# Adding a token's two expert results: the first one scaled on ScalarE and added on GpSimd, the embedding's copies on ScalarE

## The chip, the core and the metric

The kernel runs on one core of a Trainium2 chip. The metric is device time in microseconds of one execution. Before the change it is 1891.79 us, the median of three runs (1887.85 to 1893.83). Engines are named as the profile names them: PE is TensorE (PEld its weight loads), DVE is VectorE, ACT is ScalarE, POOL is GpSimd, SP is the engine that issues most DMAs.

## The reference

The program is a transformer block on 512 tokens of width 1024 (two attentions, a mixture of 32 experts, a gated per-layer embedding), and then two more layers with attention over a context. What the change touches lies where the experts' results are added and the embedding is mixed in:

```python
h = h + hier_moe(rms_norm(h, g_ffn[i]), w_rg[i], w_re[i], w1[i], w3[i], w2[i])
h = h + rms_norm(p[i] @ w_ple[i], g_ple[i]) * jax.nn.sigmoid(rms_norm(h, g_plg[i]) @ w_plg[i])
```

In `hier_moe` each token has two experts (TOP_K = 2), and its result is the sum of both expert outputs, each times the token's weight for that expert. So, for every token, h2 = h + w0*y0 + w1*y1; then the gate is a projection of the normalised h2, and u is the normalised embedding p @ w_ple.

## The kernel before

The 512 tokens are four chunks (c = 0 to 3) of 128 partitions, with the 1024 features along the free axis. The experts wrote their results to `y_d` in DRAM. When the last expert is done, `fetch(c)` (lines 1577 to 1582) gathers two tiles yk of a chunk by indirect DMAs that POOL issues, k = 0 and 1. Then a loop over chunks (lines 1586 to 1597) issues the gathers of the next chunk, adds both results into the chunk's tile h2 by two VectorE instructions (line 1591), takes the row norm (`row_norm`, line 404: a square with an accumulator on ACT at line 407, then in `rsq` a scaling on DVE at line 194 and a power on POOL at line 196), multiplies by the norm and the gain (`scaled`, line 410: tile xp), and turns xp for the matmul (`make_X`, line 381: transposes on PE at line 153, the high part Xhi on ACT at line 390, the low part Xlo on DVE at line 182). These high and low parts of a chunk, X, are what the gate's projection `b_plg` multiplies: three products per 128 features (`chunk`, line 257).

The loop also draws from a generator of filler work at line 1597. What is left there is `ple()` (line 1493): the embedding. A chunk's two halves of 512 columns come from PE into PSUM, are copied to the tiles pu (line 1502, called us in the code), squared on ACT (line 1508), and scaled on DVE (lines 1509 to 1513). The copy goes through `copy` (line 175), which counts an estimated load for ACT and DVE (`held`) and gives each copy to the one that has less. Each such copy so moves the count on which all later copies are shared out.

Each of the engines takes its instructions in a fixed order. That order is made when the program is built, by a scheduler that simulates all of it: neither the order of lines nor the engine's load at run time sets it. Beside the loop POOL has the low parts wlo of the gate's weights to make (line 251, 128x1024 each, from the high parts whi that ACT makes at line 242). The names with numbers below are buffers: h_9013 to h_9016 are the chunks 0 to 3 of h2; t_9411 and t_9418 are the two PSUM tiles of chunk 1's transposes (t_9413 and t_9420 after the change).

Of the kernel before, what the change touches and what calls it, by code (L numbers as in the profile page):

```python
# [16 lines left out]
AF = mybir.ActivationFunctionType  # L17
OP = mybir.AluOpType
# [64 lines left out]
def block_kernel(ctx: ExitStack, tc: tile.TileContext, I, out, dbg=None):  # L83
    nc = tc.nc
# [19 lines left out]
    def SM(shape, tag, dt=F32, bufs=2):  # L104
        return sm.tile(shape, dt, name=tag, tag=tag, bufs=bufs)
# [60 lines left out]
    def share(**us):  # L166

        e = min(us, key=lambda e: held[e] + us[e])
        busy(**{e: us[e]})
        return eng[e]  # L170

    def kcols(ap):
        return math.prod(ap.shape[1:]) / 1000

    def copy(o, i, on=("act", "dve")):

        us = dict(act=0.06 + 0.83 * kcols(o), dve=0.07 + 1.04 * kcols(o))
        e = share(**{n: us[n] for n in on})
        (e.copy if e is nc.scalar else e.tensor_copy)(o, i)  # L179
# [11 lines left out]
    def rsq(ssq, n, inv_n, pool=True):  # L191

        m, y, u = (SM([P, n], t, bufs=3) for t in ("rs_m", "rs_y", "rs_u"))
        nc.vector.tensor_scalar(m, ssq, inv_n, EPS, op0=OP.mult, op1=OP.add)
        if pool and n <= 4:
            nc.gpsimd.tensor_tensor(y, m, mhalf.to_broadcast([P, n]), op=OP.pow)
            return y
        nc.vector.tensor_scalar(y.bitcast(I32), m.bitcast(I32), 1, None, op0=OP.logical_shift_right)
        nc.vector.tensor_scalar(y.bitcast(I32), y.bitcast(I32), -1, 0x5F3759DF, op0=OP.mult, op1=OP.add)
        for _ in range(3):  # L200
            nc.vector.scalar_tensor_tensor(u, m, -0.5, y, op0=OP.mult, op1=OP.mult)
            nc.vector.tensor_mul(u, u, y)
            nc.vector.scalar_tensor_tensor(y, u, 1.5, y, op0=OP.add, op1=OP.mult)
        return y
# [176 lines left out]
    def make_X(y, nk, dst=None):  # L381

        hi, lo = dst or (XT([P, nk, P], F32R, name=s) for s in ("Xhi", "Xlo"))
        for k0 in range(0, nk, 4):
            kn = min(4, nk - k0)
            ps = T1()
            for k in range(kn):
                tr(ps[:, k * P:(k + 1) * P], y[:, k0 + k::nk])
            pv = ps[:, :kn * P].rearrange("p (k t) -> p k t", k=kn)
            nc.scalar.copy(hi[:, k0:k0 + kn], pv)  # L390
            sub_lo(lo[:, k0:k0 + kn], pv, hi[:, k0:k0 + kn])
        return hi, lo

    def make_Xs(ys, nk):

        per = 1024 // (nk * P)
        X = []
        for c, y in enumerate(ys):
            if c % per == 0:
                t = [Y([P, min(per, len(ys) - c), nk, P], F32R, name=s) for s in ("Xhi", "Xlo")]  # L400
            X.append(make_X(y, nk, [u[:, c % per] for u in t]))
        return ByTok(X)

    def row_norm(x, n):

        ssq = SM([P, 1], "ssq1", bufs=4)
        nc.scalar.activation(junk[:, :n], x, AF.Square, accum_out=ssq)
        return rsq(ssq, 1, 1.0 / n)

    def scaled(y, x, r, g):  # L410

        nc.vector.scalar_tensor_tensor(y, x, r, g, op0=OP.mult, op1=OP.mult)
# [1070 lines left out]
    def ple_load():  # L1483
        if not xp:
            gp.append(Y([P, D], name="gple"))
            gp.append(load_row(gp[0], I["g_ple"], D))
            for c in range(NC4):
                x = T2([P, 256], name="px")
                load(x, I["p"][rows(c), :])
                xp.append(x)  # L1490


    def ple():
        wpv = I["w_ple"].rearrange("(p c) n -> p c n", c=2)
        blks = [Dense(wpv, 2, [(b * 512, 512)]).load().split() for b in range(2)]
        ple_load()
        gp[1]()
        Xp = make_Xs(xp, 2)
        yield
        for b, d in enumerate(blks):  # L1500
            d.X = Xp
            d.evac = lambda c, ps, b=b: copy(us[c][b], ps)
        for c in range(NC4):
            us.append([(K3 if c < 3 else T2)([P, 512], name="pu") for _ in range(2)])
            ssq = SM([P, 2], "ussq")
            for b in range(2):
                blks[b].chunk(c)
                nc.scalar.activation(junk[:, :512], us[c][b], AF.Square, accum_out=ssq[:, b:b + 1])
            nc.vector.tensor_tensor(ssq[:, 0:1], ssq[:, 0:1], ssq[:, 1:2], op=OP.add)
            r = rsq(ssq[:, 0:1], 1, 1.0 / D)  # L1510
            nc.vector.tensor_scalar(r, r, 0.5, None, op0=OP.mult)
            for b in range(2):
                scaled(us[c][b], us[c][b], r, gp[0][:, b * 512:(b + 1) * 512])
            yield
# [3 lines left out]

    us, paid = [], [0]
    filler = chain(ctx_path(cx), ple())  # L1520
    last = None
    ws = {0: early[0],
# [16 lines left out]
    _, wts, yidx, oidx, ovf_e, novf = res  # L1539
# [35 lines left out]
    yks = []  # L1575

    def fetch(c):
        for k in range(2):
            yk = Y([P, D], name="yk")
            i = k * NC4 + c  # L1580
            gather(yk, y_d.rearrange("b s n -> (b s) n"), yidx[:, i:i + 1])
            yks.append(yk)
# [3 lines left out]
    for c in range(NC4):  # L1586
        h = h2[c]
        if c + 1 < NC4:
            fetch(c + 1)
        for k in range(2):  # L1590
            nc.vector.scalar_tensor_tensor(h, yks[2 * c + k], wts[:, k, c:c + 1], h, op0=OP.mult, op1=OP.add)
        dbg(f"h2_{c}", h)
        r = row_norm(h, D)
        x = Y([P, D], name="xp")
        scaled(x, h, r, gplg)
        Xt.append(make_X(x, 8))
        next(filler, None)
# [356 lines left out]
```

## Time and profile before

| | us |
|---|---|
| runs, median (lowest to highest) | 1891.79 (1887.85 to 1893.83) |
| the profiled execution, its own time | 1893.7 |
| the profiled execution, its span from first to last instruction | 1891.9 |
| PE, DVE, ACT, POOL busy | 1683.8, 933.2, 741.0, 614.2 |

The span is 1.8 us shorter than the time of the same execution. Times in the rows are counted from the start of the span, so that a stretch can be found again in each view. Busy time is a sum over the whole span. What a change is worth depends on the stretch in which it lies, and on which engine there is waited for.

### The profile page before, as it was taken

What the parts mean: (1) busy time and instruction counts of PE and PEld (TensorE: products, weight loads), DVE (VectorE), ACT (ScalarE), POOL (GpSimd) and SP (SyncE); (2) the same over time, 40 slices, a digit from 0 to 9 for tenths busy, and PEclk for the clock granted to TensorE, in tenths of its full rate; (3) what the DMA queues carried; (4) which work ended last, traced back from release to release, by engine and by line L of the source; (5) the groups of instructions that cost most, each with busy time, mean ns of one, the idle gap of its engine ahead of it and who ended that gap; (6) DMA issues with size and microseconds to landing.
All of it is one profiled execution on the core that took longest, in us unless ns stands there. A gap on an engine that the chain in (4) does not pass through costs nothing. (4 is left out here: it accounts for less than half of the span.)

```text
span 1891.9 us, 28397 instructions
## 1 busy us (share of the span) xinstructions
PE 1683.8 (89%) x10457; PEld 1204.5 (64%) x10457; DVE 933.2 (49%) x2017; ACT 741.0 (39%) x1620; POOL 614.2 (32%) x697
## 2 busy tenths in 40 slices
PE   7999878969998889898897699898989989879988
PEld 6787655756655545455553578775556977757767
DVE  5755657353223122221332865566552757786652
ACT  5344547312222212121222444255562534656660
POOL 4861223212221212122112534533123436453232
PEclk9999988979999999998898899999999989999999
DMA  8445676688999999997999533100023435421031
GB/s 238 156 175 179 203 236 202 223 320 308 377 409 400 336 382 339 358 318 263 352 409 387 193 102 116 56 1 1 1 90 122 137 122 167 123 87 56 23 134 45
DMA packets 189983, 385.34 MB, mean 204 GB/s; under 512 B 28184, under 2 KB 86136, under 8 KB 189840
## 3 DMA queue, kind: packets, MB, share of 16 engines
q1 hardware_dynamic: 186384, 375.08, 56.1%
q0 software_dynamic: 3456, 8.39, 1.4%
q8 instruction: 84, 1.38, 0.3%
q14 instruction: 59, 0.48, 0.1%
HBM read 348.86 MB, written 38.13 MB: 205 GB/s over the span
## 5 line engine op out<-in xcount | busy, mean ns | idle before, releaser
L150 PE MATMUL d<-we,exT 128*64 128x256 f32 x2048 | 254.8, 393 | 10.9 <-DMA we<-in_w 8.0
L150 PE MATMUL d<-whi,Xhi 128*128 128x512 f32 (+2 forms) x560 | 219.1, 393 | 5.9 <-DVE gsg L587 3.4
L150 PE MATMUL d<-wlo,Xhi 128*128 128x512 f32 (+2 forms) x560 | 218.7, 391 | 3.5 <-POOL wlo L251 3.5
L150 PE MATMUL d<-whi,Xlo 128*128 128x512 f32 (+2 forms) x560 | 219.2, 392 | 1.3 <-DVE Xlo L182 1.2
L251 POOL TENSOR_TENSOR wlo<-raw,whi 128x1024 fp32r<-128x1024 f32 (+2 forms) x71 | 171.3, 2432 | 139.1 <-ACT whi L242 79.7
L150 PEld LDWEIGHTS d<-we,exT 128*64 128x64 f32 x2048 | 148.0, 140 | 101.2 <-issue 25.5
L242 ACT CAST whi<-raw 128x1024 fp32r<-128x1024 f32 (+2 forms) x130 | 131.7, 1020 | 130.4 <-PE d L150 89.3
L513 DVE TENSOR_REDUCE ast<-s 128x1 f32<-128x768 f32 (+1 forms) x160 | 135.3, 848 | 92.0 <-PE s L150 90.1
L515 ACT ACTIVATE pr<-s,ast 128x768 f32<-128x768 f32 (+1 forms) x160 | 131.2, 821 | 58.1 <-DVE ast L513 54.7
L153 PE MATMUL t<-ident,pr 128*128 128x128 f32 x832 | 125.5, 283 | 13.9 <-DVE PT L179 6.8
L150 PE MATMUL s<-stk 128*128 128x256 f32 x448 | 120.4, 355 | 18.7 <-ACT pr L515 14.2
L248 POOL TENSOR_TENSOR wlo<-raw,whi 128x512 fp32r<-128x512 f32 (+2 forms) x69 | 82.2, 1221 | 145.0 <-ACT whi L242 82.9
L150 PE MATMUL d<-we,eth 128*64 128x512 f32 x512 | 122.0, 603 | 6.7 <-DVE eth L1433 6.7
L150 PEld LDWEIGHTS d<-whi,Xhi 128*128 128x128 f32 x560 | 108.2, 193 | 28.3 <-DVE gsg L587 3.6
L150 PEld LDWEIGHTS d<-wlo,Xhi 128*128 128x128 f32 x560 | 108.1, 193 | 24.3 <-POOL wlo L251 4.4
L150 PEld LDWEIGHTS d<-whi,Xlo 128*128 128x128 f32 x560 | 108.0, 193 | 22.0 <-DVE Xlo L182 2.2
L150 PE MATMUL d<-whi,ot 128*128 128x512 f32 x384 | 120.2, 392 | 1.4 <-DVE rT L1291 0.9
L153 PEld LDWEIGHTS t<-ident,pr 128*128 128x128 f32 x832 | 96.4, 144 | 37.2 <-DVE PT L179 10.9
L1425 DVE SCALAR_TENSOR_TENSOR eth<-eth,d 128x256 f32<-128x256 f32 x32 | 13.5, 421 | 169.6 <-ACT eth L1424 169.6
L150 PEld LDWEIGHTS s<-stk 128*128 128x128 f32 x448 | 70.5, 195 | 34.9 <-ACT pr L515 22.9
L1457 POOL DMA_INDIRECT xg<-xn_d,gidx x16 | 16.6, 1039 | 222.2 <-PE t L153 114.2
L150 PEld LDWEIGHTS d<-whi,ot 128*128 128x128 f32 x384 | 71.9, 188 | 18.7 <-issue 1.8
(475 smaller groups left out, 3191.8 us busy)
## 6 DMA issues: line engine op xcount, KB each, us to landing
we<-in_w SPq DMA_DIRECT2D x378, 512.0 KB
raw<-in_l_w_mod SPq DMA_DIRECT2D x48, 512.0 KB
raw<-in_l_w_in SPq DMA_DIRECT2D x64, 256.0 KB
raw<-in_w_in SPq DMA_DIRECT2D x24, 512.0 KB
raw<-in_l_w_out SPq DMA_DIRECT2D x24, 512.0 KB
raw<-in_l_w_in SPq DMA_DIRECT2D x16, 512.0 KB
y_d<-ey SPq DMA_DIRECT2D x64, 128.0 KB
bias<-bias SPq DMA_DIRECT2D x48, 128.0 KB
```

The costliest lines, as they stand in the source:

```text
L150: nc.tensor.matmul(o, l, r, start=start, stop=stop)
L153: nc.tensor.transpose(o, x, identr if x.dtype == F32R else ident)
L242: nc.scalar.copy(t, src)
L248: e.tensor_tensor(t, src[:, k], hi[k].bitcast(F32), op=OP.subtract)
L251: e.tensor_tensor(t, src, whole.bitcast(F32), op=OP.subtract)
L513: nc.vector.tensor_reduce(st[:, h:h + 1], ps, op=OP.max, axis=AX.X, negate=True)
L515: nc.scalar.activation(p, ps, AF.Exp, bias=st[:, h:h + 1], accum_out=sums[:, c, h:h + 1])
L1425: nc.vector.scalar_tensor_tensor(th[:, 256:], th[:, :256], 1.0, ps[:, :256], op0=OP.add, op1=OP.mult)
L1457: nc.gpsimd.indirect_dma_start(out=x, out_offset=None, in_=src, in_offset=bass.IndirectOffsetOnAxis(ap=idx, axis=0), bounds_check=src.shap ...
```

## The change

The copies of the embedding's halves from PSUM (8 of 128x512) go to ACT always; they no longer pass through `copy`, and so no longer count in its sharing. Of a chunk's two expert results, the first, y0, is multiplied by its weight in place on ACT, and added to h2 on POOL. The second, y1, is multiplied and added on DVE by one instruction as before.

```diff
@@ -1499,7 +1499,7 @@
         for b, d in enumerate(blks):
             d.X = Xp
-            d.evac = lambda c, ps, b=b: copy(us[c][b], ps)
+            d.evac = lambda c, ps, b=b: nc.scalar.copy(us[c][b], ps)
@@ -1587,8 +1587,10 @@
         if c + 1 < NC4:
             fetch(c + 1)
-        for k in range(2):
-            nc.vector.scalar_tensor_tensor(h, yks[2 * c + k], wts[:, k, c:c + 1], h, op0=OP.mult, op1=OP.add)
+        y0, y1 = yks[2 * c:2 * c + 2]
+        nc.scalar.activation(y0, y0, AF.Copy, scale=wts[:, 0, c:c + 1])
+        nc.gpsimd.tensor_tensor(h, h, y0, op=OP.add)
+        nc.vector.scalar_tensor_tensor(h, y1, wts[:, 1, c:c + 1], h, op0=OP.mult, op1=OP.add)
         r = row_norm(h, D)
```

In the changed kernel these lines are 1591 (scale), 1592 (add) and 1593 (the second result), and all lines behind them stand two lower.

POOL's order at the start of the loop, as a difference; cyk belongs to a side path, rs_y is the power of a norm, DMA yk a gather:

```order
 L756 TENSOR_TENSOR cyk<-cyk,g_8271 128x256 x2
 L196 TENSOR_TENSOR rs_y<-rs_m,mhalf 128x1
-L251 TENSOR_TENSOR wlo<-raw,whi 128x1024 x2
+L1592 TENSOR_TENSOR h_9013<-h_9013,yk 128x1024
+L251 TENSOR_TENSOR wlo<-raw,whi 128x1024 x2
+L1592 TENSOR_TENSOR h_9014<-h_9014,yk 128x1024
 L196 TENSOR_TENSOR rs_y<-rs_m,mhalf 128x1 x2
 L1457 DMA yk<-y_d,yidx 128x1024 x2
 L196 TENSOR_TENSOR rs_y<-rs_m,mhalf 128x1
 L1457 DMA yk<-y_d,yidx 128x1024 x2
```

The adds of chunks 0 and 1 stand around the two low parts, and all four ahead of the next powers and gathers.

DVE's order at the same place, before:

```order
L1591 SCALAR_TENSOR_TENSOR h_9013<-yk,wts,h_9013 128x1024
L179 COPY pu<-d_9428 128x512
L1591 SCALAR_TENSOR_TENSOR h_9013<-yk,wts,h_9013 128x1024
L1511 TENSOR_SCALAR rs_y<-rs_y 128x1
L1591 SCALAR_TENSOR_TENSOR h_9014<-yk,wts,h_9014 128x1024
L412 SCALAR_TENSOR_TENSOR pu<-pu,rs_y,gple 128x512 x2
L1591 SCALAR_TENSOR_TENSOR h_9014<-yk,wts,h_9014 128x1024
L194 TENSOR_SCALAR rs_m<-ssq_9335 128x1
L1509 TENSOR_TENSOR ussq<-ussq 128x1
L194 TENSOR_SCALAR rs_m<-ussq 128x1
L412 SCALAR_TENSOR_TENSOR xp<-h_9013,rs_y,gplg 128x1024
```

And after:

```order
L1511 TENSOR_SCALAR rs_y<-rs_y 128x1
L412 SCALAR_TENSOR_TENSOR pu<-pu,rs_y,gple 128x512 x2
L1593 SCALAR_TENSOR_TENSOR h_9013<-yk,wts,h_9013 128x1024
L194 TENSOR_SCALAR rs_m<-ssq_9336 128x1
L1509 TENSOR_TENSOR ussq<-ussq 128x1
L194 TENSOR_SCALAR rs_m<-ussq 128x1
L1593 SCALAR_TENSOR_TENSOR h_9014<-yk,wts,h_9014 128x1024
L412 SCALAR_TENSOR_TENSOR xp<-h_9013,rs_y,gplg 128x1024
```

The scaling of chunk 1's embedding (pu) stands ahead of chunk 0's h2 now, and chunk 1's h2 behind the two sums of norms.

DVE's order further on, after the change, where chunks 2 and 3 are added:

```order
L1593 SCALAR_TENSOR_TENSOR h_9015<-yk,wts,h_9015 128x1024
L1511 TENSOR_SCALAR rs_y<-rs_y 128x1
L412 SCALAR_TENSOR_TENSOR pu<-pu,rs_y,gple 128x512 x2
L194 TENSOR_SCALAR rs_m<-ssq_9468 128x1
L1593 SCALAR_TENSOR_TENSOR h_9016<-yk,wts,h_9016 128x1024
L182 TENSOR_TENSOR Xlo<-t_9420,Xhi 128x512
L412 SCALAR_TENSOR_TENSOR xp<-h_9015,rs_y,gplg 128x1024
```

Chunk 1's second low half (t_9420) stands behind chunk 3's h2 in both kernels; before, it stood behind xp of chunk 2 as well. Behind this place the orders differ in single neighbours only: about a dozen copies have changed between ACT and DVE in the later layers, by the count that no longer gets the embedding's copies.

## Rows read from the trace of the kernel before

**Rows 1.** The page of the profiled execution: its first line, the line of busy time by engine (us, share of the span, instructions), and the granted TensorE clock in 40 slices of 47.3 us (tenths of full speed).

```profile
span 1891.9 us, 28397 instructions
...
PE 1683.8 (89%) x10457; PEld 1204.5 (64%) x10457; DVE 933.2 (49%) x2017; ACT 741.0 (39%) x1620; POOL 614.2 (32%) x697
...
PEclk9999988979999999998898899999999989999999
```

**Rows 2.** The view of stretches: from:to in us of the span, its length, busy us and instructions of PE, its weight loads, DVE, ACT and POOL, then the granted TensorE clock, the share of the DMA engines and GB/s.

```profile
...
1060.00:1072.00 12.00, 0.21 (x1) 0.21 (x2) 11.55 (x14) 6.12 (x13) 6.82 (x6) 0.61 0.45 142
1072.00:1080.00 8.00, 6.11 (x21) 4.65 (x21) 5.30 (x9) 2.23 (x5) 6.47 (x6) 0.52 0.66 189
...
1090.00:1130.00 40.00, 38.41 (x179) 31.48 (x178) 27.50 (x29) 15.60 (x22) 15.51 (x8) 1.00 0.28 92
```

**Rows 3.** The timeline of PE from 1059 to 1092 us: start us, us, engine, line, operation, tiles, shape, count; in brackets the idle time before it and what ended that. The tile t is a transpose of a chunk's xp, d a product in the gate's projection (b_plg) or, at 1059.44, the last one of the embedding.

```profile
1059.44 0.39 PE L150 MATMUL d<-whi,Xlo 128*128 128x512 f32 x1
1071.79 1.97 PE L153 MATMUL t<-ident,xp 128*128 128x128 f32 x8 [11.96 <-DVE rs_y L1511]
...
1074.17 0.63 PE L150 MATMUL d<-wlo,Xhi 128*128 128x512 f32 x1
1076.69 1.12 PE L153 MATMUL t<-ident,xp 128*128 128x128 f32 x4 [1.89 <-DVE Xlo L182]
...
1085.24 0.50 PE L150 MATMUL d<-whi,Xlo 128*128 128x512 f32 x1 [0.51 <-DVE Xlo L182]
...
1089.63 1.22 PE L153 MATMUL t<-ident,xp 128*128 128x128 f32 x8 [1.36 <-DVE xp L412]
```

**Rows 4.** The timeline of DVE (VectorE) from 1055 to 1093 us, same columns; h is a chunk of h2, yk an expert result, pu half a chunk of the embedding.

```profile
1057.11 2.70 DVE L1591 SCALAR_TENSOR_TENSOR h<-yk,wts,h 128x1024 f32<-128x1024 f32 x1
1060.33 5.61 DVE L1591 SCALAR_TENSOR_TENSOR h<-yk,wts,h 128x1024 f32<-128x1024 f32 x1
...
1065.93 1.27 DVE L1591 SCALAR_TENSOR_TENSOR h<-yk,wts,h 128x1024 f32<-128x1024 f32 x1
1067.12 1.40 DVE L412 SCALAR_TENSOR_TENSOR pu<-pu,rs_y,gple 128x512 f32<-128x512 f32 x2
1068.44 1.27 DVE L1591 SCALAR_TENSOR_TENSOR h<-yk,wts,h 128x1024 f32<-128x1024 f32 x1
1069.64 0.14 DVE L194 TENSOR_SCALAR rs_m<-ssq 128x1 f32<-128x1 f32 x1
...
1069.88 0.15 DVE L194 TENSOR_SCALAR rs_m<-ussq 128x1 f32<-128x1 f32 x1
1070.45 1.28 DVE L412 SCALAR_TENSOR_TENSOR xp<-h,rs_y,gplg 128x1024 f32<-128x1024 f32 x1 [0.41 <-POOL rs_y L196]
...
1074.75 1.28 DVE L412 SCALAR_TENSOR_TENSOR xp<-h,rs_y,gplg 128x1024 f32<-128x1024 f32 x1 [1.24 <-POOL rs_y L196]
...
1081.92 2.66 DVE L1591 SCALAR_TENSOR_TENSOR h<-yk,wts,h 128x1024 f32<-128x1024 f32 x2 [2.43 <-DMA yk<-y_d,yidx]
```

**Rows 5.** The timeline of POOL (GpSimd) from 1055 to 1080 us, same columns; two instructions of a kind in a row are joined (x2).

```profile
1057.27 1.45 POOL L756 TENSOR_TENSOR cyk<-cyk,g 128x256 f32<-128x256 f32 x2
1058.66 1.57 POOL L196 TENSOR_TENSOR rs_y<-rs_m,mhalf 128x1 f32<-128x1 f32 x1
1060.21 4.64 POOL L251 TENSOR_TENSOR wlo<-raw,whi 128x1024 fp32r<-128x1024 f32 x2
1069.86 1.07 POOL L196 TENSOR_TENSOR rs_y<-rs_m,mhalf 128x1 f32<-128x1 f32 x2 [5.01 <-DVE ussq L1509]
1071.10 1.57 POOL L1457 DMA_INDIRECT yk<-y_d,yidx  x1 [0.17 <-POOL rs_y L196]
1072.98 1.13 POOL L1457 DMA_INDIRECT yk<-y_d,yidx  x1 [0.31 <-issue]
1074.13 0.58 POOL L196 TENSOR_TENSOR rs_y<-rs_m,mhalf 128x1 f32<-128x1 f32 x1
```

**Rows 6.** The timeline of POOL once more, at 1036 us and from 1123 to 1132 us: one low part made with VectorE idle beside it, and two of them in a row.

```profile
1036.60 2.34 POOL L251 TENSOR_TENSOR wlo<-raw,whi 128x1024 fp32r<-128x1024 f32 x1 [2.50 <-ACT whi L242]
...
1124.35 5.82 POOL L251 TENSOR_TENSOR wlo<-raw,whi 128x1024 fp32r<-128x1024 f32 x2 [2.79 <-ACT whi L242]
```

**Rows 7.** The timeline of DVE from 1123 to 1132 us, beside the two low parts of rows 6.

```profile
1123.40 1.22 DVE L251 TENSOR_TENSOR wlo<-raw,whi 128x1024 fp32r<-128x1024 f32 x1
1124.54 3.42 DVE L665 TENSOR_TENSOR ly<-ly,mrow 128x1024 f32<-128x1024 f32 x1
1127.87 2.84 DVE L1611 TENSOR_TENSOR h<-h,pth 128x512 f32<-128x512 f32 x1
```

**Rows 8.** The timeline of ACT (ScalarE) from 1066 to 1068 us, same columns.

```profile
1066.33 1.06 ACT L407 ACTIVATE junk<-h 128x1024 bf16<-128x1024 f32 x1 [4.93 <-DVE rs_y L1511]
1067.29 0.19 ACT L407 ACTIVATION_READ_ACCUMULATOR junk<-h 128x1 f32 x1
1067.51 0.63 ACT L1508 ACTIVATE junk<-pu 128x512 bf16<-128x512 f32 x1
```

**Rows 9.** The groups by line of the whole span, shapes kept apart: line, engine, operation, tiles, shape, count, busy us, mean ns of one, then the idle time of the engine ahead of them and what ended it.

```profile
L179 ACT COPY pu<-d 128x512 f32<-128x512 f32 x4 | 2.3, 586 | 2.1 <-PE d L150 2.1
...
L1591 DVE SCALAR_TENSOR_TENSOR h<-yk,wts,h 128x1024 f32<-128x1024 f32 x8 | 16.0, 1996 | 2.5 <-DMA yk<-y_d,yidx 2.4
...
L179 DVE COPY pu<-d 128x512 f32<-128x512 f32 x4 | 2.7, 685 | 0.2 <-PE d L150 0.2
```

## The prediction

> **What bounds the kernel now.** First the page: TensorE is busy for 1683.8 of 1891.9 us, all other engines for under half, so the span moves only where PE waits [rows 1]. The chain of waits reaches back only to 1140.70 us, behind the place of the change, so I read this place from the timelines, engine by engine. PE ends the embedding's last product at 1059.44 + 0.39 and stands still for 11.96 us, until chunk 0's xp is there for the transposes at 1071.79; then it waits 1.89 us for chunk 1's, 0.51 for a low part and 1.36 for xp of chunk 2 [rows 3]. From 1090 to 1130 us it is busy for 38.41 of 40 us [rows 2]. What these four waits (15.72 us) gain or lose is therefore carried to the end.
>
> What fills the 11.96 us? DVE: y0 of chunk 0 in 2.70 us, y1 in 5.61, chunk 1's two in 1.27 each, and pu between [rows 4]. Undisturbed such an instruction takes 1.27; the group's mean of 1.996 [rows 9] is no price of work. POOL makes two low parts beside them (1060.21, 4.64 us together) [rows 5]. One alone is 2.34 us [rows 6], so these two ran undisturbed and DVE's 5.61 is waiting: 1060.33 + 5.61 = 1065.94, which is 1.09 behind POOL's end at 1064.85. The two engines take turns where both read two tiles.
>
> How they do so decides this change. At 1124.35 two low parts take 5.82 us [rows 6], 1.14 more than 2 x 2.34, while a DVE addition beside them takes 3.42 and the next 2.84 [rows 7]: DVE waits to the end of the low part that runs, then gets in, and the next low part is longer by DVE's turn. At 1060.33 DVE was passed over at that boundary and waited through both.
>
> By the Trainium skill ("SBUF — State Buffer", "Who interferes with whom") a DVE instruction with two inputs in SBUF and a GpSimd instruction that reads SBUF lock each other out, for the whole instruction, and whoever issues first has the ports. The turns at 1124 agree. By that rule alone the 5.61 would have ended at about 1063.6, one boundary earlier; the row shows more than the rule.
>
> **The change, part by part.** *Removed from DVE*: four additions at 1.28 and four pu copies at 0.685 [rows 4, 9], less one gplg copy that goes to it: 5.1 + 2.7 - 0.7 = 7.2 us. Of this only what lies before 1070.45 could count, and there DVE waits for POOL anyway.
>
> *Added to ACT*: four copies at 0.586 [rows 9] and four scalings of 128x1024; none is in the trace, the nearest row is the square at 1.06 us [rows 8], so 1.1 each, in all 6.1 us after the gplg copy is off. ACT had 4.93 us idle ahead of 1066.33 [rows 8], and chunk 0's scaling can be done at about 1058, when POOL still has cyk and a power before it. I cost it at nothing. Bounds: 0, and 2 x 1.1 if that cover is gone (chunks 0 and 1 both late for POOL). No gain below nothing: it is work added.
>
> *Added to POOL*: four additions of 128x1024, two inputs in SBUF. The trace has no such addition on POOL; nearest is the low part of the same size, 2.34 us alone [rows 6]. I take that. Lower bound 1.27, DVE's own time for that size; upper 2.91, half of 5.82. These stand on the path: chunk 0's before both low parts, chunk 1's behind them, and all ahead of the powers and of chunk 2's two gathers.
>
> *Moved on DVE*: pu of chunk 1 stands before chunk 0's h2, and chunk 1's h2 behind the two sums of norms. So chunk 0's xp waits for DVE's h2 of chunk 1, and that waits for ACT.
>
> The sum for chunk 0 by turns: POOL's power ends at 1057.27 + 1.45 + 0.58 [rows 5], some 0.2 later because a copy on ACT delays what leads to it: 1059.5. POOL adds chunk 0's y0 until 1061.8; DVE scales half of pu (0.70) to 1062.5; low part to 1064.8; second half to 1065.5; low part to 1067.8; DVE adds y1 to 1068.9, where before it was 1065.94. POOL adds chunk 1's y0 to 1071.25. ACT squares h2 and two halves of pu: 1.25 + 2 x 0.82 with their accumulators [rows 8], 1071.8. DVE's small sums 0.14 + 0.15 and gaps [rows 4], 1072.2; chunk 1's y1, 1.27, 1073.5; xp, 1.28, 1074.8. PE begins at 1074.8, where before it was 1071.79: **+3.0**.
>
> *Second wait.* POOL's next power (0.58) ends at 1073, two gathers (1.57 + 0.31 + 1.13) and a power (0.58) [rows 5] end at 1076.6, chunk 1's xp, with issue, at 1078.1 instead of 1076.03 [rows 4]. PE, by then 3.0 late, would have been at the transposes at 1077.8 less its 1.89 of waiting: it waits less, and its shift there is **+1.5**. The TensorE clock stands here: 0.61 and 0.52 were granted from 1060 to 1080, after PE stood still [rows 2], and 1.00 from 1090. The longer stop and the shorter second one leave that as it is, so I charge nothing; bound +1.0 (a product is 0.63 us at 1074.17 against 0.39 [rows 3]: four more of them at the low level).
>
> *Third.* The gathers of chunk 2 go out 2 us later. DVE's h2 additions at 1081.92 waited 2.43 for a gather [rows 4], so chunk 2's y1 is added at 1083.9, ends at 1085.2. Then chunk 3: POOL's addition ends at 1089.1 (waiting for the gathers, then 2.34 and turns), DVE's at 1090.4, and behind it on DVE stands chunk 1's second low half, 1091.1; xp of chunk 2 comes next. PE's transposes of chunk 2 come at 1093.4 against 1089.63, +3.8. But in the new order about ten products of chunk 1 stand before them, 38.41 / 179 = 0.21 us each [rows 2], 2.2 us of work that PE had left to do later; and its waits on the late low half cost about 1.2. **+2.8 - 0.1**, so the sum at the end is **+2.7**.
>
> *Later layers.* About a dozen copies of at most 0.7 us change engine by the count. No row of this stretch prices this. PE runs there mostly without a wait [rows 1, 2]; I take 0, bounds -4 and +4: half a dozen copies at 0.685 on the path to either side.
>
> So span 1894.6, profiled execution 1893.7 + 2.7 = 1896.4. The median of the runs is 1.9 below that execution: **1894.5 us**. A measurement of this kernel can tell about 0.3% from no change, 5.7 us: below 1886.1 or above 1897.5.
>
> A rule speaks against the whole move: the Trainium skill ("Perfetto Trace Analysis", "Optimizing Scalar/DVE Operations") says that GpSimd and DVE share a read port, so that shifting work between them might not help. The sum above says the same from the rows: a DVE turn of 1.27 becomes a POOL turn of 2.34 that DVE must wait for.
>
> **The rivals.** *Passed over (slower).* If DVE loses every boundary in this train, as it did at 1060.33 [rows 4], four POOL instructions run unbroken, 1059.5 + 4 x 2.34 = 1068.9; pu twice (1.40) and y1 (1.27) follow, 1071.5; with 1.25 + 1.64 + 0.3 + 1.27 + 1.28 PE begins at 1077.3, +5.5, and one more lost turn at chunk 3's addition makes +6.5: **1898.3 us**. It decides from +5.7, so two lost boundaries and one more. For it: both rows of 2.70 and 5.61 lie in this very stretch. Against: at 1124 DVE got in at each boundary [rows 6, 7].
>
> *POOL alone bounds (faster).* If DVE's turns fit beside POOL's (pu ready before the train begins, additions shorter than 2.34), chunk 0's h2 is ready early and only POOL's 1068.9 + 0.6 counts: y1 of chunk 1 ends at 1070.2, xp at 1071.5, -0.3; the later waits of 0.51 and 1.36 [rows 3] vanish, since DVE has 7.2 us less to do: -2.2, **1889.6 us**. For it: relief of DVE, which is busy for 5.30 of 8 us at 1072 [rows 2]. Against: DVE's wait for POOL is most of its time there. All of the idle, 15.72, caps any gain.
>
> *Copies outweigh.* The copies shared out anew decide the sign, and the place matters little: **1887 to 1899 us**, middle 1893.
>
> **How the numbers follow.** By turns 0.45 (a change of +2.7, own range 1891 to 1898); passed over 0.22; POOL alone 0.20; copies 0.13. Faster by over 0.3%: a fifth of POOL alone, a third of copies, little of the rest: 0.11. Slower by over 0.3%: six tenths of passed over, a seventh of by turns, a third of copies: 0.25. Within: 0.64. The range goes from the low end of POOL alone with copies in its favour, 1887, to passed over with the clock's and copies' share, 1901.
>
> **What would show it.** In the profile after: PE's wait before the first transposes 15 us instead of 11.96 (step one); low parts longer than 2.34 with pu's turns between; DVE's y1 of chunk 0 ending near 1068.9; xp of chunk 1 near 1078; chunk 2's transposes near 1093.4, behind more products of chunk 1. It is wrong if DVE's pu or y1 waits over a boundary (passed over), if PE begins at or before 1071.8 (POOL alone), if POOL's addition is far from 2.34, or if the stretch up to 1095 shifts by one amount and the end by another (copies).

## The result and the profile after

The changed kernel takes 1910.25 us, the median of four runs (1907.12 to 1915.15), beside 1892.81 (four runs now, three before the prediction) for the kernel before: ratio 1.0096, 95% interval 1.0075 to 1.0117, so 14 to 22 us slower. The forecast was 1894.5 with a range from 1887 to 1901. The profiled execution took 1915.15 us.

The page of the changed kernel, with the lines that answer to [rows 1]:

```profile
span 1913.4 us, 28411 instructions
...
PE 1699.3 (89%) x10457; PEld 1213.5 (63%) x10457; DVE 927.7 (48%) x2005; ACT 746.6 (39%) x1632; POOL 621.0 (32%) x701
```

DVE is busy for 5.5 us less than before, ACT for 5.6 and POOL for 6.8 more; the prediction had 7.2 and 6.1 for the first two. (Busy time counts an instruction from start to end, so it includes what the instruction waits inside, such as the 10.20 us below.) The span is 21.5 us longer all the same. To see where, I compared the starts of the same matmul, by its number, in both traces (10457 in each). The table gives what each stretch of the program added to PE's delay against the first trace of the kernel before, in us; the stretches are named by that trace's times.

| trace | to 1059 | place, to 1095 | to 1512 | to 1526 | to 1626 | to the end | all behind the place |
|---|---|---|---|---|---|---|---|
| changed | +1.6 | +4.8 | +4.3 | +3.2 | +3.7 | +3.8 | +15.0 |
| changed, second trace | +9.3 | +4.1 | +0.5 | +3.1 | +3.9 | +1.1 | +8.6 |
| changed, third trace | +1.9 | +6.0 | +1.5 | +3.2 | +4.0 | +3.7 | +12.4 |
| before, second trace | -6.8 | +0.2 | -1.8 | 0.0 | -1.3 | +0.3 | -2.8 |

Up to 1048 us each engine has the same instructions in the same order in both kernels, and PE has them up to its stop at the place. The first column moves by at most 1.9 us behind 1048, so the rest of it is chance: the experts' part differs by 16 us between executions. The other columns are known better: the two traces of the kernel before differ there by at most 1.8 in one stretch and by 2.8 in the last column. The place costs 4 to 6 us, and the later layers, for which the prediction took 0 with bounds of 4, cost 9 to 15.

**The place.** PE's timeline, answering to [rows 3]:

```profile
1078.09 1.97 PE L153 MATMUL t<-ident,xp 128*128 128x128 f32 x8 [16.64 <-DVE rs_y L1511]
...
1083.10 1.12 PE L153 MATMUL t<-ident,xp 128*128 128x128 f32 x4 [1.76 <-DVE rs_m L194]
...
1094.70 0.50 PE L150 MATMUL d<-whi,Xlo 128*128 128x512 f32 x1 [0.50 <-DVE Xlo L182]
...
1097.13 1.05 PE L153 MATMUL t<-ident,xp 128*128 128x128 f32 x8
```

The wait before the first transposes is 16.64 us instead of 11.96. POOL's timeline of the same stretch, answering to [rows 5]:

```profile
1060.31 0.56 POOL L196 TENSOR_TENSOR rs_y<-rs_m,mhalf 128x1 f32<-128x1 f32 x1
1060.85 2.34 POOL L1592 TENSOR_TENSOR h<-h,yk 128x1024 f32<-128x1024 f32 x1
1063.16 4.63 POOL L251 TENSOR_TENSOR wlo<-raw,whi 128x1024 fp32r<-128x1024 f32 x2
1067.76 2.33 POOL L1592 TENSOR_TENSOR h<-h,yk 128x1024 f32<-128x1024 f32 x1
...
1075.71 1.54 POOL L196 TENSOR_TENSOR rs_y<-rs_m,mhalf 128x1 f32<-128x1 f32 x1 [1.16 <-DVE rs_m L194]
...
1090.21 2.51 POOL L1592 TENSOR_TENSOR h<-h,yk 128x1024 f32<-128x1024 f32 x1 [2.71 <-ACT yk L1591]
```

DVE's timeline, answering to [rows 4]:

```profile
1061.10 10.20 DVE L412 SCALAR_TENSOR_TENSOR pu<-pu,rs_y,gple 128x512 f32<-128x512 f32 x2
1071.22 1.27 DVE L1593 SCALAR_TENSOR_TENSOR h<-yk,wts,h 128x1024 f32<-128x1024 f32 x1
...
1075.55 1.28 DVE L1593 SCALAR_TENSOR_TENSOR h<-yk,wts,h 128x1024 f32<-128x1024 f32 x1
1076.75 1.28 DVE L412 SCALAR_TENSOR_TENSOR xp<-h,rs_y,gplg 128x1024 f32<-128x1024 f32 x1
...
1092.76 1.28 DVE L1593 SCALAR_TENSOR_TENSOR h<-yk,wts,h 128x1024 f32<-128x1024 f32 x1 [1.40 <-POOL h L1592]
1093.96 0.68 DVE L182 TENSOR_TENSOR Xlo<-t,Xhi 128x512 fp32r<-128x512 f32 x1
```

Read the two side by side. POOL's addition, two low parts and second addition take 2.34, 4.63 and 2.33 us, nothing more than alone, one right behind the other from 1060.85 to 1070.09: this is POOL's *train*. DVE's two scalings of pu, 1.40 in [rows 4], take 10.20: the first got its turn only when POOL was through, 1.2 us ahead of their joint end at 1071.30. It was passed over at three boundaries out of three. That is the rival "passed over", to the row. Behind it y1 of chunk 0 (1071.22), ACT's squares, y1 of chunk 1 (1075.55) and xp (1076.75) follow as in the sum. At the end of the stretch DVE's addition of chunk 3 waits 1.40 for POOL's, and chunk 1's last low half (1093.96) stands behind it; PE waits 0.50 for that half at 1094.70. The cover of the new work on ACT held, as ACT's timeline shows:

```profile
1058.11 1.16 ACT L1591 ACTIVATE yk<-yk,wts 128x1024 f32<-128x1024 f32 x1 [0.77 <-DMA yk<-y_d,yidx]
...
1060.11 1.06 ACT L242 CAST whi<-raw 128x1024 fp32r<-128x1024 f32 x1
1062.48 1.15 ACT L1591 ACTIVATE yk<-yk,wts 128x1024 f32<-128x1024 f32 x1 [1.32 <-DMA yk<-y_d,yidx]
```

The first scaling (1.16 us) ended at 1059.27, 1.6 us before POOL could use it.

The view of stretches, answering to [rows 2]:

```profile
1062.00:1078.00 16.00, 0.00 (x0) 0.00 (x0) 13.34 (x9) 6.23 (x11) 10.75 (x7) 0.64 0.29 95
1078.00:1086.50 8.50, 6.59 (x20) 4.97 (x21) 4.97 (x11) 4.21 (x9) 7.67 (x6) 0.50 0.70 192
1096.00:1136.00 40.00, 37.72 (x176) 30.81 (x174) 26.91 (x28) 15.43 (x22) 15.15 (x8) 1.00 0.28 92
```

The clock is low at the same place: 0.64 and 0.50 after PE stood still, 1.00 from 1096.

**The later layers.** The largest wait that is new stands at 1526 us (1512 to 1526 in the table), where the second layer's query latent yqa is normalised. PE's timeline of the changed kernel there:

```profile
1532.64 1.52 PE L153 MATMUL t<-ident,yqa 128*128 128x128 f32 x6 [5.99 <-DVE yqa L412]
```

ACT's timeline just ahead of it (whi is a weight's cast, junk a square):

```profile
1525.19 1.05 ACT L242 CAST whi<-raw 128x1024 fp32r<-128x1024 f32 x1 [5.23 <-DMA raw<-in_l_w_in]
1526.14 0.52 ACT L1744 ACTIVATE junk<-yqa 128x384 bf16<-128x384 f32 x1
...
1526.66 0.46 ACT L179 COPY yqa<-d 128x384 f32<-128x384 f32 x1
1527.15 0.52 ACT L1744 ACTIVATE junk<-yqa 128x384 bf16<-128x384 f32 x1
```

The low part on DVE that frees a buffer:

```profile
1518.92 2.36 DVE L251 TENSOR_TENSOR wlo<-raw,whi 128x1024 fp32r<-128x1024 f32 x1
```

The DMA queue (SPq), which fills that buffer:

```profile
1521.30 0.37 SPq L129 DMA_DIRECT2D raw<-in_l_w_in  x1
```

In the kernel before, PE's timeline at the same transposes:

```profile
1517.17 1.11 PE L153 MATMUL t<-ident,yqa 128*128 128x128 f32 x6 [1.28 <-DVE yqa L412]
```

Its ACT:

```profile
1508.77 0.49 ACT L179 COPY yqa<-d 128x384 f32<-128x384 f32 x1
...
1510.67 1.06 ACT L242 CAST whi<-raw 128x1024 fp32r<-128x1024 f32 x1 [0.60 <-DMA raw<-in_l_w_in]
```

And its DMA queue:

```profile
1507.07 0.37 SPq L129 DMA_DIRECT2D raw<-in_l_w_in  x1
```

Before, a copy of yqa and its square on ACT are done ahead of a weight's cast, which waits 0.60 us for its DMA. After, the cast waits 5.23, and two squares and the last copy are queued behind it; PE waits 5.99 instead of 1.28 (the prediction's rows do not reach here). The DMA went out at 1507.07 before, just when POOL's low part freed a buffer; after, at 1521.30, just when DVE's low part (1518.92 + 2.36) did. (POOL's low part, 1504.63 + 2.41, ended at 1507.04.) Nobody edited this code: four copies of yqa went to DVE, ACT, DVE, ACT where they had gone to ACT, DVE, ACT, DVE, and in the order that follows the transfer got another buffer. The section on the change says that behind the place the orders differ in single neighbours only. That is too little: compared by names, some 5% of PE's instructions behind 1130 us and 10 to 12% of DVE's and ACT's stand outside the longest order that both kernels share.

### The profile page after: what moved, and what is told of

Same layout as the page of the kernel before. It is cut to its first block, busy times and chain, and to the rows that moved or that the text cites. A ratio compares the mean times of both kernels' runs of the same rounds, so it can differ in the third digit from the quotient of the medians.

```text
span 1913.4 us, 28411 instructions
## 1 busy us (share of the span) xinstructions
PE 1699.3 (89%) x10457; PEld 1213.5 (63%) x10457; DVE 927.7 (48%) x2005; ACT 746.6 (39%) x1632; POOL 621.0 (32%) x701
## 5 line engine op out<-in xcount | busy, mean ns | idle before, releaser
L150 PE MATMUL d<-we,exT 128*64 128x256 f32 x2048 | 259.2, 398 | 9.7 <-DMA we<-in_w 6.8
L1457 POOL DMA_INDIRECT xg<-xn_d,gidx x16 | 16.6, 1036 | 223.2 <-PE t L153 114.6
```

The source lines that it names most:

```text
L150: nc.tensor.matmul(o, l, r, start=start, stop=stop)
L1457: nc.gpsimd.indirect_dma_start(out=x, out_offset=None, in_=src, in_offset=bass.IndirectOffsetOnAxis(ap=idx, axis=0), bounds_check=src.shap ...
```

## The experiments

Theory after the result: the loss has two parts, the **place** (POOL's train keeps DVE out) and the **sharing** (the count without the embedding's copies shares out all later copies in another way). Rival: the place carries all, and the later stretches are chance. The runs are called e1 to e16; differences in us are worked out from the ratios.

**1. Sharing alone (e1, and once more as e14).** The kernel before; the copies go where they went, uncounted.

```diff
-            d.evac = lambda c, ps, b=b: copy(us[c][b], ps)
+            d.evac = lambda c, ps, b=b: (nc.scalar.copy if (c < 2) == (b == 0) else nc.vector.tensor_copy)(us[c][b], ps)
```

> The kernel before, in which the embedding's eight copies go to the engines that they went to before (half to ACT, half to DVE), but no longer count in the sharing; nothing else is edited. The additions stand as before. Sharing theory (most of the loss is in the later layers, because every later copy is shared out by another count): PE keeps its time up to 1130 us and loses 9 to 13 us behind 1400 us; 1902 to 1906 us where the kernel before has 1893. Place theory (the expert additions and the copies' own move carry the loss, the later layers differ only by chance): 1893, within 3 us of the kernel before.

> The kernel before with the copies where they were, but uncounted, a second time. Parts that add up: 5 to 9 us over the kernel before. If its first measurement (6.8) was low by chance: 10 us or more.

Ratios 1.0036 (1.0016 to 1.0055) and 1.0074 (1.0053 to 1.0095): +6.8 and +14.0 us, with no instruction of the experts' results touched. The two intervals (3 to 10 and 10 to 18 us) barely meet.

**2. All but the sharing (e2, and once more as e15).** The changed kernel; the copies on ACT count as before.

```diff
-            d.evac = lambda c, ps, b=b: nc.scalar.copy(us[c][b], ps)
+            d.evac = lambda c, ps, b=b: (share(act=0.06 + 0.83 * 0.512, dve=0.07 + 1.04 * 0.512), nc.scalar.copy(us[c][b], ps))
```

> The changed kernel, in which the embedding's copies go to ACT but are counted as before, so that later copies are shared out as in the kernel before. Sharing theory: only the loss at the place is left, PE's first transposes of xp 5 us later than before and the end 4 to 7 us later; 1897 to 1900 us. Place theory: the whole loss, 1907 to 1913 us.

> The changed kernel with the copies counted as before, a second time. Parts that add up: 3 to 6 us over the kernel before. If its first measurement (3.6) was low by chance: 8 us or more.

Ratios 1.0019 (1.0001 to 1.0036) and 1.0042 (1.0021 to 1.0063): +3.6 and +7.9 us.

**3. The copies' move (e3), and the additions' move (e4), each alone.** The kernel before with the copies on ACT, uncounted; and the changed kernel with the copies through `copy` as before.

> The kernel before with the embedding's copies on ACT, uncounted; both expert results added on DVE as before. Sharing theory: like the kernel with the uncounted copies alone, 1902 to 1906 us, with the stretch up to 1130 us within 1 us of before. Place theory: 1890 to 1895 us, since the additions are not moved.

> The changed kernel with the embedding's copies shared out as before; only the first expert result's scaling and addition move (ACT, POOL). Sharing theory: 1897 to 1900 us, all of it at the place, PE's first transposes 4 to 6 us later. Place theory: 1907 to 1913 us.

Ratios 1.0051 (1.0030 to 1.0071) and 1.0017 (0.9999 to 1.0035).

**4. The changed kernel again (e5, e13)**, and (e16) with the copies on their former engines, uncounted (the first diff's lambda in the changed kernel).

> The changed kernel once more, beside the runs of the kernel before on this chip, for a second trace. Sharing and place add up: place +4 to +5 (first transposes of xp), later layers +7 to +10, so 11 to 15 us over the kernel before. What the first trace showed beyond that (16 products of the context attention at 1437 us at the low clock, and 8 more at the end) is chance if this trace doesn't have it, and belongs to the change if it has it again.

> The changed kernel a third time, on one chip with the three that follow. If the parts add up (place 4 to 5, later layers 6 to 9): 11 to 14 us over the kernel before, and the part ahead of the place within 5 us of its other traces to either side. If the parts together cost more than their sum: 17 us or more again, and the trace shows in which stretch.

> The changed kernel, but the embedding's copies stay where they were before (half on DVE) and are uncounted: new sharing and the moved addition, without the copies' own move. Parts that add up: 10 to 14 us over the kernel before, place +4 to +5, later layers +8 to +10. If the copies on ACT are what makes the whole dearer than its parts: 5 us or more below the changed kernel on the same chip.

Ratios 1.0116 (1.0090 to 1.0142), 1.0097 (1.0077 to 1.0117) and, for the last, 1.0098 (1.0079 to 1.0117). After the first two groups it was open whether the parts (10.4 us) could make the whole (18.2 and 21.9). On the chip of e13 to e16 they do within their intervals, though all four came out above what was expected: 14.0 + 7.9 against 18.3 us for the whole, and with 18.5 for e16 the copies' own move to ACT is not needed for it. By stretch, as in the first table:

| trace | place | to 1512 | to 1526 | to 1626 | to the end | all behind the place |
|---|---|---|---|---|---|---|
| e1, e14 sharing alone | -0.3, 0.0 | +1.5, +3.2 | +3.3, +3.1 | +3.6, +4.7 | +0.5, +0.4 | +9.0, +11.5 |
| e3 copies only | +0.6 | +2.6 | +3.3 | +3.4 | +0.6 | +9.9 |
| e16 additions, new sharing | +5.7 | +1.3 | +3.1 | +3.5 | +0.6 | +8.4 |
| e2, e15 all but sharing | +4.4, +4.9 | -0.2, -0.6 | +0.2, +0.6 | -0.6, -1.4 | +3.1, -0.9 | +2.6, -2.3 |
| e4 additions only | +5.2 | -1.1 | +0.3 | +1.2 | +1.7 | +2.0 |

In this table and the first, every trace with the additions moved has +4.1 to +6.0 at the place and the others at most 0.6; every one with the new sharing has +3.1 to +3.3 at yqa and +3.4 to +4.7 behind it, the others at most 0.6 and 1.2. The new sharing also costs in the stretch up to 1512, between 1319 and 1447 us: +3.1 to +3.6 in six of its seven traces and +6.6 in the changed kernel's first, -0.2 to +0.3 in the other four. The rival falls.

The stretch up to 1626 has its new stop at 1618 us of the changed kernel. PE's timeline:

```profile
1618.22 0.51 PE L153 MATMUL d<-identr,stg 128*128 128x128 f32 x4 [2.83 <-DVE sg L587]
```

And DVE's, just ahead of it:

```profile
1615.57 0.97 DVE L426 TENSOR_TENSOR yq<-yq,rope_t 128x128 f32<-128x128 f32 x1
1616.46 1.01 DVE L627 CAST stg<-stg 128x128 fp32r<-128x128 f32 x1
```

PE did not wait at these transposes before. The two DVE instructions run beside three low parts on POOL (1615.35 to 1618.35); in the kernel before, ahead of such low parts, they took 0.29 and 0.22 us. All seven traces with the new sharing have this row of DVE (0.96 to 0.97, 1.01) and a wait of 2.5 to 3.3 us on PE. So here too DVE stands behind POOL; no experiment varied it alone.

What the changed kernel's first trace had beyond this (+4.3 up to 1512; +6.6 between 1319 and 1447 where the others have 3.1 to 3.6) was a low clock. PE's timeline of the first trace, at 16 products of the second layer:

```profile
1437.24 5.94 PE L150 MATMUL d<-PT,gvx 128*64 128x512 f32 x16 [1.03 <-DVE PT L179]
```

Its stretches there:

```profile
1437.00:1444.00 7.00, 6.76 (x22) 2.17 (x24) 0.18 (x1) 2.76 (x3) 3.88 (x2) 0.65 0.56 200
```

PE's timeline of the second trace, at the same products:

```profile
1442.67 3.65 PE L150 MATMUL d<-PT,gvx 128*64 128x512 f32 x16 [1.49 <-DVE PT L179]
```

And its stretches:

```profile
1442.60:1447.00 4.40, 4.33 (x20) 1.49 (x22) 0.02 (x1) 2.52 (x3) 1.74 (x1) 1.00 0.86 314
```

The same 16 products took 5.94 us at a granted clock of 0.65 and 3.65 at 1.00, behind much the same waits. The last stretch has such a place too: 24 products near the end took 7.07 us at 0.74 in the third trace and 5.37 at 1.00 in the second, and the stretch +3.7 and +1.1.

**5. One site of the sharing (e6).** The changed kernel with the four copies of yqa on their former engines, counted as any copy.

```diff
-        copy(yqa[c], ps)
+        share(act=0.06 + 0.83 * 0.384, dve=0.07 + 1.04 * 0.384)
+        (nc.vector.tensor_copy if c % 2 else nc.scalar.copy)(yqa[c], ps)
```

> The changed kernel with only the four copies of yqa (128x384) put on the engines that they had before (chunks 0 and 2 ACT, 1 and 3 DVE, counted as any copy). Theory of the late copy: in the changed kernel the last of them stands on ACT behind a weight's cast that waits 5.2 us for its DMA, and that DMA waits for VectorE's low part to free its buffer; with the four in the old order PE's wait before the transposes of yqa is 1 to 2 us instead of 6 and the shift there is gone: 3 to 4 us less at this place, all else as in the changed kernel. Rival (the transfer is late for another reason): PE waits 5 to 6 us as before.

PE's timeline of this kernel at the transposes of yqa:

```profile
1521.76 1.11 PE L153 MATMUL t<-ident,yqa 128*128 128x128 f32 x6 [1.14 <-DVE yqa L412]
```

Its ACT, at the weight's cast:

```profile
1515.33 1.05 ACT L242 CAST whi<-raw 128x1024 fp32r<-128x1024 f32 x1 [0.54 <-DMA raw<-in_l_w_in]
```

Ratio 1.0059 (1.0038 to 1.0080). PE waits 1.14 us, ACT's cast 0.54; this stretch went from +3.2 to -0.2, and the ones around it stayed (+3.4 before it, +4.5 behind). The runs as a whole came out 11 us below the changed kernel on the same chip (e5), more than this site is worth; the stretches of the two traces from the place on do not show the rest (+12.9 beside +12.7), and it is not explained.

**6. Another count (e12).** The kernel before with one line more ahead of the loop, `busy(act=0.5)`.

> The kernel before with 0.5 us added to ACT's count once, ahead of the loop; no instruction is added or moved by hand. Sharing theory in its general form (the later layers have a good order by luck of the count, and any shift of it deals the copies anew): the later layers move by 2 us or more to either side, place unchanged; likeliest 3 to 9 us slower. Rival (only the change's own shift is harmful): within 2 us of the kernel before.

PE's timeline of this kernel at the same transposes:

```profile
1518.02 1.31 PE L153 MATMUL t<-ident,yqa 128*128 128x128 f32 x5 [6.16 <-DVE yqa L412]
```

Its ACT, at the weight's cast:

```profile
1510.56 1.05 ACT L242 CAST whi<-raw 128x1024 fp32r<-128x1024 f32 x1 [5.01 <-DMA raw<-in_l_w_in]
```

Its DVE, at the last copy of yqa:

```profile
1509.13 0.56 DVE L179 COPY yqa<-d 128x384 f32<-128x384 f32 x1 [1.97 <-PE d L150]
```

Ratio 1.0045 (1.0023 to 1.0066): half a microsecond in a counter that no engine sees costs 8.5 us. Here the last copy of yqa stands on DVE (1509.13) as before the change, and PE waits 6.16 all the same, since the cast waits 5.01 for its DMA. So it is the late transfer, not the place of the copy, that costs at this site; the theory of experiment 5 had the link right and its first cause wrong. Other stretches moved to both sides (-3.1 up to 1512).

**7. What lets DVE in (e7, e8).** Kernel before, and kernel of experiment 2, with the embedding's norm on DVE, so that no power stands ahead of POOL's train.

```diff
-            r = rsq(ssq[:, 0:1], 1, 1.0 / D)
+            r = rsq(ssq[:, 0:1], 1, 1.0 / D, pool=False)
```

> The kernel before, with the embedding's norm computed on DVE in small steps and no longer by a power on POOL, so that POOL's two low parts at 1060 us no longer follow a power without a gap. Theory of the power: all of the trains in which DVE was passed over start right behind a power; without it DVE gets in at the boundary, the second addition of chunk 0 ends 2 us earlier (3 to 3.5 us instead of 5.6) and PE's wait is 10 us instead of 12; 1891 to 1893 where the kernel before has 1894. Rival (passing over depends on DVE's instruction, not on what POOL did before): an addition is passed over again, at least 5 us, no gain.

> The changed kernel with the old sharing (copies counted) and, as in the run without the power, the embedding's norm on DVE. Theory of the power: the train of four on POOL has DVE's turns in between, the scaling of pu no longer takes 10.2 us for two but under 6, POOL's train takes 10 to 11.5 us instead of 9.3, and the loss at the place falls from 4.4 to about 2 to 3 us. Rival: pu waits through the whole train again, 9 to 10 us, loss as in the run with the power.

POOL's timeline of e7, at the two low parts of the place:

```profile
1061.04 5.86 POOL L251 TENSOR_TENSOR wlo<-raw,whi 128x1024 fp32r<-128x1024 f32 x2 [3.05 <-issue]
```

DVE's timeline of e7 beside them:

```profile
1061.42 3.28 DVE L1591 SCALAR_TENSOR_TENSOR h<-yk,wts,h 128x1024 f32<-128x1024 f32 x1
1064.62 2.30 DVE L201 SCALAR_TENSOR_TENSOR rs_u<-rs_m,rs_y 128x1 f32<-128x1 f32 x1
```

PE's timeline of e7 at the place, two of its waits:

```profile
1071.97 1.97 PE L153 MATMUL t<-ident,xp 128*128 128x128 f32 x8 [9.48 <-DVE xp L412]
...
1084.89 0.51 PE L150 MATMUL d<-whi,Xlo 128*128 128x512 f32 x1 [2.05 <-DVE Xlo L182]
```

DVE's timeline of e8 beside POOL's train, the first of four such steps:

```profile
1058.67 2.35 DVE L201 SCALAR_TENSOR_TENSOR rs_u<-rs_m,rs_y 128x1 f32<-128x1 f32 x1
```

In e7 DVE got in: y1 of chunk 0 took 3.28 us instead of 5.61, though the norm's next small step then waited 2.30. PE's first wait fell from 11.96 to 9.48 us, as the theory had it. But the gain was gone by the end of the place (-0.4; ratio 1.0029, 1.0010 to 1.0048): PE, early by then, waited 2.05 us (0.51 in [rows 3]) for a low half that stands on DVE behind additions waiting for their gathers (idle 3.63 at 1081.63), and 2.00 for another at 1095.43. In e8 four steps of one column each waited a whole POOL instruction (2.26 to 2.35): place +7.3, ratio 1.0056 (1.0036 to 1.0077), against my +2 to +3. A VectorE instruction that takes 0.16 us alone (1067.95) pays the full turn.

**8. A shorter train (e9, e10).** Kernel before, and kernel of experiment 2, with three of the gate's low parts on DVE (the line that sets `dve_los` to empty for all others is left out).

```diff
...
-                e = nc.vector if lo_flip[0] % lo_mod[0] == 0 else nc.gpsimd
+                e = nc.vector if lo_flip[0] % lo_mod[0] == 0 or len(self.sp) in self.dve_los else nc.gpsimd
...
+    b_plg[0].dve_los, b_plg[1].dve_los = (2, 3), (0,)
```

> The kernel before with three low parts of the gate's weights (the last two of its first half, the first of its second half) made on DVE and not on POOL; everything else as before. Lock-out theory (the place waits because POOL's low parts keep DVE out): no instruction of POOL of 2.3 us stands in the loop's first stretch, chunk 0's additions end at 1061 instead of 1065.9, PE's wait before the first transposes is 8 to 9 us instead of 12, and 3 to 6 us are gained at the end: 1886 to 1889 where the kernel before has 1892. Rival (the gathers or the norm's chain are late anyway): PE's wait stays at 11 to 12 us, no gain.

> The changed kernel with the old sharing (copies counted) and with the same three low parts on DVE: POOL's train is only the two additions. Lock-out theory: DVE is kept out for 4.7 us instead of 9.3, PE's first transposes come 1 to 2 us earlier than in the kernel before instead of 4.4 later, and the additions on POOL still cost 2 to 3 us against the same kernel with them on DVE. Rival (it is the order of DVE, chunk 1 ahead of chunk 0's xp, that costs): the loss at the place stays at 3 to 5 us.

PE's timeline of e9 at the place:

```profile
1076.36 1.97 PE L153 MATMUL t<-ident,xp 128*128 128x128 f32 x8 [9.68 <-DVE rs_m L194]
...
1083.89 1.12 PE L153 MATMUL t<-ident,xp 128*128 128x128 f32 x4 [4.52 <-DVE rs_m L194]
```

POOL's timeline of e9, at chunk 2's gathers:

```profile
1075.16 2.08 POOL L1457 DMA_INDIRECT yk<-y_d,yidx  x1 [0.17 <-POOL rs_y L196]
1077.54 0.99 POOL L1457 DMA_INDIRECT yk<-y_d,yidx  x1 [0.31 <-issue]
1078.56 1.10 POOL L196 TENSOR_TENSOR rs_y<-rs_m,mhalf 128x1 f32<-128x1 f32 x2
```

POOL's timeline of e10, at its two additions:

```profile
1063.86 5.12 POOL L1593 TENSOR_TENSOR h<-h,yk 128x1024 f32<-128x1024 f32 x2
```

DVE's timeline of e10 beside them:

```profile
1064.10 5.43 DVE L412 SCALAR_TENSOR_TENSOR pu<-pu,rs_y,gple 128x512 f32<-128x512 f32 x2
```

With the same addition on POOL, the place is now 1.7 us shorter than before instead of 4.4 longer, and no worse than e9, where the additions are on DVE (-1.2). I had expected e10 to be 2 to 3 us worse than e9. So the moved addition is dear here only in a train with the low parts. e9's first wait fell to 9.68, but 2.6 us came back in the second (4.52 against 1.89 in [rows 3]): chunk 1's power now stands behind chunk 2's gathers (1075.16, 1077.54) on POOL. Both kernels were slower than before (1.0043, 1.0026 to 1.0060; 1.0047, 1.0031 to 1.0062); their traces have +5.7 and +3.9 behind the place. No version here beats the kernel before.

e10 also refutes the theory of the power: its train starts right behind a power (1063.32 to 1063.88), and DVE got in (POOL's two took 5.12). A reading that fits most trains: DVE is passed over where the input of POOL's next instruction was ready before the present one started (in the changed kernel ACT's cast ended at 1061.17 and the scaling at 1063.63, the low parts started at 1063.16 and 1065.46), and gets in where it came later (in e10 the scaling began at 1064.97, behind the first addition's start at 1063.86; in e7 the cast began at 1061.17, behind the low part's at 1061.04). It does not fit e8, nor the power of 1.57 us in [rows 5]: its input was ready at 1057.19, before POOL's instruction ahead of it began (1057.96), and DVE's addition got in all the same. No experiment varied it alone; it is open.

**9. The kernel before again (e11).**

> The kernel before itself, for a second trace: how far the stretches of one kernel differ between two executions. Up to 1050 us (the experts) 3 us or more either way; at the place and in each stretch of the later layers under 0.7 us, except where a stretch meets the low clock; from 1800 to 1820 us 2 us more than in the first trace, since six other kernels, with either sharing, have that there.

The waits of [rows 3] came back as 11.91, 1.88, 0.26 and 1.36. The stretches of the later layers differed by up to 1.8, more than the 0.7 that I had expected; from 1800 to 1820 us it had 1.8 more than the first trace, as expected.

## Why the prediction was wrong

The direction, slower, was right; the size and the range failed by two steps that were both named, one as a rival and one as a bound, and were taken for alternatives where they add up.

- *Turns at the boundaries.* The sum gave DVE a turn at each boundary of POOL's train, by the rows at 1124 us [rows 6, 7], and set aside the two rows of this very stretch that said otherwise [rows 4, 5]. With the 1.6 us by which the trace was late already, chunk 0's y1 ended at 1070.9 (forecast 1068.9; the rival 1071.5), and PE began at 1076.5 (1074.8; the rival 1077.3).
- *Second wait.* PE's second transposes came 6.4 us later than before, 4.8 without the 1.6 (forecast +1.5): the stop was 1.76 beside 1.89, not shorter. Most of this followed from the first step. But the sum also took one power ahead of chunk 2's gathers where [rows 5] have two (x2); the second waited for the embedding's squares and took 1.54 us beside DVE's addition (1075.71). And in both traces this stop ends with a low half (Xlo) behind xp, not with xp: xp was done at 1082.37, the transposes began at 1083.10.
- *Third wait.* That chunk 1's products would stand ahead of chunk 2's transposes, and chunk 1's last low half behind chunk 3's addition, was right; the transposes began at 1097.13 - 1.6 = 1095.5 (forecast 1093.4). The place ended at +4.8 (forecast +2.7, rival +6.5); traces 2 and 3 have +4.1 and +6.0.
- *Prices.* POOL's addition 2.34, ACT's scaling 1.16 (1.1), and the cover on ACT were right. The clock, put at nothing, cost little: from PE's restart it stood at 0.50 for 7.9 us before (1071.80 to 1079.70), for 8.7 in the first trace of the changed kernel (1078.10 to 1086.80) and for 10.5 in the third (1078.60 to 1089.10). At half speed that is some 0.4 and 1.3 us, an estimate; the bound was 1.0.
- *Later layers.* The bound of 4 us was half a dozen copies at their own duration. That is the wrong unit: a copy that changes engine moves the order, and with it a transfer's buffer, and one such move cost 3.2 us at yqa; at sg, where VectorE stands behind POOL's low parts, PE waits another 2.83. The runs with the sharing alone (e1, e14) put this term at 7 to 14 us, their traces at 9.0 and 11.5.
- *Two rules beside the rows.* By the Trainium skill ("SBUF — State Buffer", "Who interferes with whom") one instruction holds the shared ports to its end; the rows show POOL keeping them through four, 9.3 us. The rule of the Trainium skill ("Perfetto Trace Analysis", "Optimizing Scalar/DVE Operations"), that moving work between GpSimd and DVE might not help, holds at the place (+4.1 to +6.0); in e10, where no low part stands in the train, the move did no harm (-1.7).

## What to carry to other kernels

Before moving work to GpSimd, look at what will stand next to it on that engine: a VectorE instruction may have to wait for one of GpSimd's instructions (2.3 us for 0.16 in e8) or for a whole train (10.20 for 1.40 in the changed kernel), however short it is itself. The runs show this for instructions with two SBUF inputs, and at 1616 us for a cast. An edit that changes a counter, a cost or an order for the whole program is not local; price it by what it can make wait elsewhere (transfers, queues), or keep the counter as it was, and test the two apart. Where single executions differ by as much as the effect, compare traces stretch by stretch.

## What the runs showed that I had not expected

The same two low parts let VectorE in or not, 5.61 or 3.28 us for one addition, and what decides it is open. And 0.5 us added to a planner's count slowed the kernel by 0.45% (0.23 to 0.66) without moving an instruction by hand. A stop in the later layers, which no line of the change touches, had GpSimd's low parts ahead of VectorE once more.
